# The first norm of a two-layer trunk: row factors before the transposes, gain column behind them

## The chip, the cores and the metric

One NeuronCore of one Trainium2 chip. The metric is device time in microseconds (us) of one execution, median over runs. Engines are named as the profile names them: PE (matmul), PEld (its weight loads), DVE (vector), ACT (scalar), POOL (GpSimd), SP (which issues the DMAs).

## The reference, cut to what matters

```python
def rms_norm(x, gain):
    x32 = x.astype(jnp.float32)
    y = x32 * lax.rsqrt(jnp.mean(x32 * x32, axis=-1, keepdims=True) + RMS_EPS) * gain
    return y.astype(x.dtype)

def swiglu(h, w_gate, w_up, w_down):
    return (jax.nn.silu(h @ w_gate) * (h @ w_up)) @ w_down

h = x                                       # (1, 256, 1024) float32
for layer in range(2):
    g = norm_gain[layer]
    f = swiglu(rms_norm(h, g[0]), w_gate[layer, 0], w_up[layer, 0], w_down[layer, 0])
    h = h + 0.5 * rms_norm(f, g[1])
    ...                                     # a mixer (pooling, or attention), then a second swiglu
```

The width is 1024, the inner width of a swiglu 2816. Only the very first `rms_norm(h, g[0])` and what its output feeds are touched here; four swiglu stages, a pooling mixer, a key/value projection and an attention mixer follow unchanged.

## The kernel before, in words

The 256 tokens are two tiles of 128 rows, `h[0]` and `h[1]`. A float32 product is made of three fast ones: each operand is split into a high part (rounded to the matmul's type) and a low part (the rest), and high·high, high·low and low·high are summed in PSUM. ACT makes the high part, DVE subtracts it to get the low part, both for the weights (`parts` on 1024 columns, lines 99 and 100; `form` on 2048 columns, lines 106 and 107) and for the activations.

A norm is computed with tokens on partitions: ACT squares and sums a row (line 174), DVE adds the two half sums (line 176), POOL raises to the power -1/2 (line 178), DVE multiplies by the gain, which a DMA has spread over all partitions (line 255), and by the row's factor (lines 256 and 260, or ACT on line 258). PE then transposes eight blocks of 128x128 into two PSUM banks of four blocks (`transposed`, line 203); per bank ACT writes the high part (line 205) and DVE the low part (line 206) into `aT`, whose layout is (high or low, block of 128 columns, token).

`Sums` makes four differences of quarters of the transposed activations, split again into parts: the swiglu's products for columns 512 to 2559 use seven half-size products in place of eight, and take these sums as one operand (`st<-hl_hi,S_x`). Before, `add_half` copies three of the four PSUM quarters to SBUF on ACT (line 230), and DVE subtracts (lines 233 to 240); `parts` of that class splits each result (lines 244 and 245).

The first stage of the first swiglu multiplies `aT` by eight weight units (`units`, 1024 columns each, named u0 to u7 below): 96 matmuls into four accumulators `acc_b`, 24 for each token tile and each of gate and up. u0 to u3 are the gate's, u4 to u7 the up's. They come in 1 MB tiles `raw` of two units; three such tiles exist, so the fourth load waits for DVE to have split the first. A unit of index q is multiplied with blocks 2q and 2q+1 of `aT` (modulo four units). Then `pair(1, ...)` begins with the product `g`, from a tile split by `form`.

A scheduler orders most instructions. In the block around the first norm the order of DVE and ACT is that of the code (`manual_schedule`), so an instruction that waits holds up all behind it on its engine. PE's order is the scheduler's. Ahead of all this 64 matmuls on zeros keep PE busy (line 81).

Of the kernel before, what the change touches and what calls it, by code (L numbers as in the profile page):

```python
# [23 lines left out]
NF = FF // P  # L24
KC = D // P
# [5 lines left out]
EPS = 1e-6  # L31
# [13 lines left out]


@with_exitstack
def trunk_kernel(ctx: ExitStack, tc: tile.TileContext, x, pos, gains, pscale, ws, wq, invf, amask, pmat, icnt, out):
# [10 lines left out]
    sc4 = ctx.enter_context(tc.tile_pool(name="sc4", bufs=2))  # L59
    sc2 = ctx.enter_context(tc.tile_pool(name="sc2", bufs=7))  # L60
    sc1 = ctx.enter_context(tc.tile_pool(name="sc1", bufs=1))
    st = ctx.enter_context(tc.tile_pool(name="st", bufs=4))
    accp = ctx.enter_context(tc.tile_pool(name="accp", bufs=4, space=PSUM))
    gup = ctx.enter_context(tc.tile_pool(name="gup", bufs=2, space=PSUM))
    tpp = ctx.enter_context(tc.tile_pool(name="tpp", bufs=2, space=PSUM))

    h = [cp.tile([P, D], F32, name=f"h{i}") for i in range(2)]
    for k in range(2):
        nc.sync.dma_start(h[0][:, k * 512 : (k + 1) * 512], x[0:P, k * 512 : (k + 1) * 512])
    first_units = []  # L70

    ident = cp.tile([P, P], F32, name="ident")
    make_identity(nc, ident)
    nhalf = cp.tile([P, 1], F32, name="nhalf")
# [11 lines left out]
    def load_raw(pool=rawp, tag="raw", raw=None, at=None):  # L86

        b = block_no[0]
        raw = pool.tile([P, 2, 1024], F32, tag=tag, name=f"{tag}{b}") if raw is None else raw
        for k in range(2) if at is None else (at,):  # L90
            last["dma"] = nc.sync.dma_start(raw[:, k], ws[b, :, k * 1024 : (k + 1) * 1024])
        block_no[0] += at != 0
        return raw

    def parts(raw, k, n=1024, xy=False):

        pool, tag = (xyp, "xy") if xy else (hlp, "hl")
        hl = pool.tile([P, 2, 1024], F32R, tag=tag, name="hl")
        nc.scalar.copy(hl[:, 0, :n], raw[:, k, :n])  # L99
        last["dve"] = nc.vector.tensor_sub(hl[:, 1, :n], raw[:, k, :n], hl[:, 0, :n])  # L100
        return hl[:, 0], hl[:, 1]
# [68 lines left out]
    def rstd_of(halves, name):  # L170
        ss = st.tile([P, 2], F32, tag="ss", name=f"ss_{name}")
        for k in range(2):
            jk = sc1.tile([P, 512], BF16, tag="junk", bufs=1, name=f"jk_{name}{k}")
            nc.scalar.activation(jk, halves[k], AF.Square, scale=1.0 / 32.0, accum_out=ss[:, k : k + 1])
        ms = st.tile([P, 1], F32, tag="ms", name=f"ms_{name}")
        nc.vector.scalar_tensor_tensor(ms, ss[:, 0:1], EPS, ss[:, 1:2], op0=ALU.add, op1=ALU.add)
        rs = st.tile([P, 1], F32, tag="rs", name=f"rs_{name}")
        nc.gpsimd.tensor_tensor(rs, ms, nhalf, op=ALU.pow)
        return rs
# [17 lines left out]
    def transposed(i, src, dst, name, sums=None):  # L197

        for b in range(2):
            tp = tpp.tile([P, 4, P], F32, tag="tp", name=f"tp_{name}{i}{b}")  # L200
            for c in range(4):
                k = b * 4 + c
                nc.tensor.transpose(tp[:, c], src[:, k * P : (k + 1) * P], ident)
            d = dst[:, :, b * 4 : b * 4 + 4, i * P : (i + 1) * P]
            nc.scalar.copy(d[:, 0], tp)  # L205
            nc.vector.tensor_sub(d[:, 1], tp, d[:, 0])
            if sums is not None:
                sums.tp[i, b] = tp

    class Sums:  # L210
# [15 lines left out]
        def add_half(self, i, b, tp):  # L226
            a = self.a
            if (i, b) != (1, 1):
                a[i, b] = self.tmp(f"{i}{b}")
                nc.scalar.copy(a[i, b], tp)  # L230
            if (i, b) == (1, 0):
                s3 = self.tmp("s")
                nc.vector.tensor_sub(s3, a[0, 0], tp)
                self.parts(2, s3)
            if (i, b) == (1, 1):
                nc.vector.tensor_sub(a[1, 0], tp, a[1, 0])
                self.parts(0, a[1, 0])
# [3 lines left out]
                self.parts(3, a[0, 1])  # L241

        def parts(self, k, src):
            nc.scalar.copy(self.out[:, k, 0], src)
# [2 lines left out]
    def row_rstd(i, name):  # L247
        return rstd_of([h[i][:, 0:512], h[i][:, 512:1024]], f"q{name}{i}")

    def norm(i, gain, name, rs=None, split=True):  # L250
        rs = row_rstd(i, name) if rs is None else rs
        y = sc4.tile([P, D], F32, tag="y", name=f"n_{name}{i}")
        for k in range(2):
            c = slice(k * 512, (k + 1) * 512)
            nc.vector.tensor_mul(y[:, c], h[i][:, c], gain[:, c])
        nc.vector.tensor_scalar_mul(y[:, 0:512], y[:, 0:512], rs)
        if split:
            nc.scalar.mul(y[:, 512:1024], y[:, 512:1024], rs)
        else:
            nc.vector.tensor_scalar_mul(y[:, 512:1024], y[:, 512:1024], rs)  # L260
        return y
# [4 lines left out]
    def new_aT(name):  # L266
        return atp.tile([P, 2, KC, S], F32R, tag="aT", name=f"aT_{name}")

    def acc_pair(name):
        return [accp.tile([P, 512], F32, tag="acc", name=f"acc_{name}{k}") for k in range(2)]  # L270
# [232 lines left out]
    ivf = cp.tile([P, 32], F32, name="ivf")  # L503
# [33 lines left out]
    aT = go.aT  # L537
# [9 lines left out]
    raw = rawp.tile([P, 2, 1024], F32, tag="raw", name="rawpm")  # L547
# [62 lines left out]
    f = [acc_pair(f"w{i}") for i in range(2)]  # L610
# [38 lines left out]
    aT = go.aT  # L649
# [20 lines left out]
    for g in range(3):  # L670
        units = load_units(4, g % 2 == 0)
        for i in range(2):
# [3 lines left out]
            tp = tpp.tile([P, 4, P], F32, tag="tp", name=f"ktp{g}{i}")  # L676
# [285 lines left out]
```

## Time and profile before

| | us |
|---|---|
| median of three runs | 984.12 (982.98 to 987.3) |
| the profiled execution | 985.76 |
| its span | 984.0 |
| PE busy in the span | 950.4 |
| DVE, ACT, POOL busy in the span | 684.1, 542.9, 62.3 |

The span is from the first to the last instruction on the chip; 1.76 us of the execution lie around it. PE is busy for 97% of the span, so the time that a change at the start can gain or lose is what it does to the moment from which PE runs without a gap, and to later gaps. Busy is not the same as fast: the profile gives for every stretch the clock that PE was granted (PEclk, 1.00 is full speed).

### The profile page before, as it was taken

To read this page: it belongs to the slowest core of one execution; us is meant where nothing else is said; L and a number is where in the kernel's file an instruction comes from. 1 tells how busy PE (TensorE), PEld (TensorE's weight loads), DVE (VectorE), ACT (ScalarE), POOL (GpSimd) and SP (SyncE) were. 2 spreads that over 40 slices of the span, in tenths; PEclk is the share of its full clock that TensorE was granted. 3 is DMA by queue.
4 is the path that set the end of the run, shared out by engine and by line. 5 is a ranking of instruction groups with operands and counts; after the bars stand their busy time and mean duration, and the time that the engine had idled before them with its cause. 6 is when DMAs were issued, how large, how long until landed. Compare 5 with 4: busy or idle time off the path is not lost.

```text
span 984.0 us, 12092 instructions
## 1 busy us (share of the span) xinstructions
PE 950.4 (97%) x4560; PEld 783.7 (80%) x4560; DVE 684.1 (70%) x771; ACT 542.9 (55%) x693; POOL 62.3 (6%) x66
## 2 busy tenths in 40 slices
PE   7999999999999999999999999999987899999997
PEld 6888788878788878877888888788976778887886
DVE  5979874577788886458887964785465587887642
ACT  6665753455657565347656743644345576665531
POOL 0000000000100000000000000100033310000000
PEclk8999999999999999999999999999999799999999
DMA  7886876475468687546687765564324236967721
GB/s 248 286 266 205 259 260 207 173 227 187 164 211 265 181 280 261 179 139 213 153 317 218 268 243 175 177 217 139 127 95 153 86 107 194 330 163 260 247 90 43
DMA packets 55898, 197.16 MB, mean 200 GB/s; under 512 B 7392, under 2 KB 7392, under 8 KB 53792
## 3 DMA queue, kind: packets, MB, share of 16 engines
q1 hardware_dynamic: 53456, 179.35, 52.2%
q0 software_dynamic: 2384, 17.04, 8.9%
q8 instruction: 36, 0.59, 0.2%
q14 instruction: 22, 0.18, 0.0%
HBM read 178.54 MB, written 1.05 MB: 183 GB/s over the span
## 4 chain that ended last, share of the span: by engine, by line
PE 74%; DVE 11%; ACT 5%; DMA 4%; issue 3%; POOL 2%; SPq 0%; POOLq 0%; DVEq 0%; ACTq 0%
PE acc_d L127 22%; PE g L127 12%; PE st L314 12%; PE u L127 7%; PE acc_b L127 6%; PE vp L127 3%; DVE hl L100 3%; PE kp L127 3%; DMA xy<-raw 2%; DVE hl_lo L107 2%; PE htp L295 2%; ACT hl L99 2%; PE qp L127 1%; DVE h L193 1%; PE acc_w L127 1%
## 5 line engine op out<-in xcount | busy, mean ns | idle before, releaser
L100 DVE TENSOR_TENSOR hl<-raw,hl 128x1024 fp32r<-128x1024 f32 x182 | 221.0, 1222 | 111.6 <-ACT hl L99 110.5
L99 ACT CAST hl<-raw 128x1024 fp32r<-128x1024 f32 x182 | 189.7, 1051 | 138.3 <-PE acc_d L127 103.3
L127 PE MATMUL acc_d<-hl,h 128*128 128x512 f32 x1056 | 243.5, 390 | 0.0
L127 PEld LDWEIGHTS acc_d<-hl,h 128*128 128x128 f32 x1056 | 197.3, 188 | 40.4
L107 DVE TENSOR_TENSOR hl_lo<-xy,hl_hi 128x2048 fp32r<-128x2048 f32 x40 | 91.6, 2291 | 48.6 <-ACT hl_hi L106 48.6
L107 DVE TENSOR_TENSOR hl_lo<-raw,hl_hi 128x2048 fp32r<-128x2048 f32 x48 | 109.4, 2285 | 15.6 <-ACT hl_hi L106 15.5
L106 ACT CAST hl_hi<-xy 128x2048 fp32r<-128x2048 f32 x40 | 76.5, 1913 | 64.0 <-DVE xy L333 29.7
L106 ACT CAST hl_hi<-raw 128x2048 fp32r<-128x2048 f32 x48 | 91.9, 1914 | 20.8 <-PE st L314 10.6
L127 PE MATMUL acc_b<-hl,aT_m 128*128 128x512 f32 x192 | 44.8, 392 | 0.3 <-ACT aT_m L205 0.3
L127 PEld LDWEIGHTS acc_b<-hl,aT_m 128*128 128x128 f32 x192 | 35.7, 188 | 8.3 <-ACT aT_m L205 0.8
L127 PE MATMUL g<-hl_hi,aT_m 128*128 128x512 f32 x128 | 41.9, 393 | 0.0
L127 PE MATMUL u<-hl_hi,aT_m 128*128 128x512 f32 x128 | 41.8, 393 | 0.0
L314 PE MATMUL st<-hl_hi,S_m 128*128 128x512 f32 x128 | 41.8, 393 | 0.0
L127 PE MATMUL qp<-hl,aT_f 128*128 128x384 f32 x192 | 38.9, 354 | 0.0
L297 ACT CAST h<-htp 128x512 fp32r<-128x512 f32 (+1 forms) x48 | 26.2, 548 | 20.0 <-PE htp L295 20.0
L127 PEld LDWEIGHTS qp<-hl,aT_f 128*128 128x128 f32 x192 | 34.8, 198 | 1.3 <-issue 0.8
L127 PE MATMUL kp<-hl,aT_hk 128*128 128x512 f32 x144 | 34.6, 394 | 0.0
L331 POOL DMA_DIRECT2D xy<-raw x16 | 14.1, 878 | 305.2 <-DVE xy L333 82.3
L127 PE MATMUL vp<-hl,aT_hk 128*128 128x512 f32 x144 | 33.1, 390 | 0.0
L314 PE MATMUL st<-hl_hi,aT_m 128*128 128x512 f32 x96 | 31.6, 393 | 1.3 <-ACT hl L99 0.9
L721 POOL TENSOR_SCALAR p<-p,rd 128x512 f32<-128x512 f32 x16 | 24.9, 1566 | 121.9 <-DVE rd L720 100.1
L298 DVE TENSOR_TENSOR h<-htp,h 128x512 fp32r<-128x512 f32 (+1 forms) x48 | 30.6, 640 | 1.1 <-ACT h L297 1.0
(246 smaller groups left out, 1596.4 us busy)
## 6 DMA issues: line engine op xcount, KB each, us to landing
raw<-in_ws SPq DMA_DIRECT2D x278, 512.0 KB, 4.8
xy<-in_ws SPq DMA_DIRECT2D x32, 512.0 KB, 6.8
xy<-raw POOLq DMA_DIRECT2D x16, 1024.0 KB, 8.1
rawq<-in_wq SPq DMA_DIRECT2D x8, 768.0 KB, 4.7
gain_post<-in_gains SPq DMA_DIRECT2D x14, 256.0 KB, 5.0
gain_pre<-in_gains SPq DMA_DIRECT2D x12, 256.0 KB, 6.1
rawpm<-in_pmat SPq DMA_DIRECT2D x2, 512.0 KB, 4.1
out_dram<-h SPq DMA_DIRECT2D x4, 256.0 KB, 2.1
```

The lines of the kernel that those rows point to most:

```text
L99: nc.scalar.copy(hl[:, 0, :n], raw[:, k, :n])
L100: last["dve"] = nc.vector.tensor_sub(hl[:, 1, :n], raw[:, k, :n], hl[:, 0, :n])
L106: nc.scalar.copy(hi, raw)
L107: last["dve"] = nc.vector.tensor_sub(lo, raw, hi)
L127: nc.tensor.matmul(o, l, r, start=start, stop=stop)
L193: nc.vector.scalar_tensor_tensor(h[i][:, c], y[:, c], rs, h[i][:, c], op0=ALU.mult, op1=ALU.add)
L295: nc.tensor.transpose(tp[:, k], prod[c, i][:, k * P : (k + 1) * P], ident)
L297: nc.scalar.copy(d[:, 0], tp[:, :nt])
L298: nc.vector.tensor_sub(d[:, 1], tp[:, :nt], d[:, 0])
L314: nc.tensor.matmul(ps, a(z, k), u[v], start=start and k == 0 and n == 0, stop=k == 3 and n == 2, skip_group_check=not start,)
L331: nc.gpsimd.dma_start(dst, src, accum_op=ALU.add)
L721: nc.gpsimd.tensor_scalar_mul(p, p, rd)
```

## The change

The gain of the first norm comes as a column: `gcol` holds 128x8 values, one column for each block, so that it is a factor per partition after the transposes. DVE multiplies `h` by the row factor alone (`first_rows`); `first_transposed` then works block by block: ACT writes the high part of transposed block times gain, DVE the low part with one scalar_tensor_tensor. The squares of a tile are summed half on ACT, half on DVE (`first_rstd`). `add_parts` builds the four quarters for the sums not from PSUM but from the high and low parts in `aT`, with four additions on POOL; the subtractions stay on DVE, and all four now read SBUF. SP's order is written out too.

```diff
+    gcol = cp.tile([P, KC], F32, name="gcol")
+    nc.sync.dma_start(gcol, gain0)          # gains[0].reshape(KC, P).T
...
+        def add_parts(self, aT):
+            a = self.a
+            for i in range(2):
+                for b in range(2):
+                    a[i, b] = self.tmp(f"{i}{b}")
+                    d = aT[:, :, b * 4 : b * 4 + 4, i * P : (i + 1) * P].bitcast(F32)
+                    nc.gpsimd.tensor_add(a[i, b], d[:, 0], d[:, 1])
+            nc.vector.tensor_sub(a[1, 1], a[1, 1], a[1, 0])
+            self.parts(0, a[1, 1])
+            nc.vector.tensor_sub(a[1, 0], a[0, 0], a[1, 0])
+            self.parts(2, a[1, 0])
...
-    gpre = load_gain(0, "pre")
+    def first_rstd(i):
+        ss = st.tile([P, 2], F32, tag="ss", name=f"ss_x{i}")
+        for k in range(2):
...
+            if k == 0:
+                nc.scalar.activation(jk, h[i][:, c], AF.Square, scale=1.0 / 32.0, accum_out=ss[:, 0:1])
+            else:
+                nc.vector.tensor_tensor_reduce(
+                    jk, h[i][:, c], h[i][:, c], 1.0 / 1024.0, 0.0, op0=ALU.mult, op1=ALU.add, accum_out=ss[:, 1:2]
+                )
...
+    def first_rows(i, rs):
+        y = sc4.tile([P, D], F32, tag="y", name=f"n_x{i}")
+        for k in range(2):
+            c = slice(k * 512, (k + 1) * 512)
+            nc.vector.tensor_scalar_mul(y[:, c], h[i][:, c], rs)
+        return y
+
+    def first_transposed(i, y):
+        for b in range(2):
...
+                nc.tensor.transpose(tp[:, c], y[:, k * P : (k + 1) * P], ident)
+            d = aT[:, :, b * 4 : b * 4 + 4, i * P : (i + 1) * P]
+            for c in range(4):
+                g = gcol[:, b * 4 + c : b * 4 + c + 1]
+                nc.scalar.mul(d[:, 0, c], tp[:, c], g)
+                nc.vector.scalar_tensor_tensor(
+                    d[:, 1, c], tp[:, c], g, d[:, 0, c].bitcast(F32), op0=ALU.mult, op1=ALU.subtract
+                )
...
-    with tc.manual_schedule(engines={mybir.EngineType.DVE, mybir.EngineType.Activation}):
-        y = norm(0, gpre, "x")
+    with tc.manual_schedule(engines={mybir.EngineType.DVE, mybir.EngineType.Activation, mybir.EngineType.SP}):
         raws = [load_raw(at=0)]
-        first_units += [parts(raws[0], 0, xy=True)]
+        load_raw(at=1, raw=raws[0])
         nc.sync.dma_start(h[1], x[P:, :])
-        transposed(0, y, aT, "x", sums)
-        rs = row_rstd(1, "x")
-        load_raw(at=1, raw=raws[0])
-        first_units += [parts(raws[0], 1, xy=True)]
-        y = norm(1, gpre, "x", rs, False)
         raws.append(load_raw())
-        first_units += [parts(raws[1], 0)]
-        transposed(1, y, aT, "x", sums)
-        first_units += [parts(raws[1], 1)]
-    for i in range(2):
-        sums.add(i)
+        rs = first_rstd(0)
+        u0 = xyp.tile([P, 2, 1024], F32R, tag="xy", name="hl")
+        nc.scalar.copy(u0[:, 0], raws[0][:, 0])
+        y = first_rows(0, rs)
+        nc.vector.tensor_sub(u0[:, 1], raws[0][:, 0], u0[:, 0])
+        first_transposed(0, y)
+        u1 = parts(raws[0], 1, xy=True)
+        rs = first_rstd(1)
+        u2 = parts(raws[1], 0)
+        y = first_rows(1, rs)
+        first_transposed(1, y)
+        first_units += [(u0[:, 0], u0[:, 1]), u1, u2, parts(raws[1], 1)]
+    sums.add_parts(aT)
```

How the change moves the queues is seen in the programs' orders, engine by engine. First DVE, from the low part of u1 to that of u3, before (`raw_199` holds u0 and u1, `raw_237` u2 and u3; names after "waits" are the engines or DMA semaphores that must have counted up):

```order
L100 TENSOR_TENSOR hl<-raw_199,hl 128x1024 [waits DMAHW6_49,Activation_49]
L255 TENSOR_TENSOR n_x_232<-h_101,gain_pre_178 128x512 [waits DMAHW5_49]
L255 TENSOR_TENSOR n_x_232<-h_101,gain_pre_178 128x512
L256 TENSOR_SCALAR n_x_232<-n_x_232,rs_qx_226 128x512 [waits DVE_49,Pool_49]
L260 TENSOR_SCALAR n_x_232<-n_x_232,rs_qx_226 128x512 [waits DVE_49]
L100 TENSOR_TENSOR hl<-raw_237,hl 128x1024 [waits DMAHW7_49,Activation_49]
L206 TENSOR_TENSOR aT_x<-tp_x_243,aT_x 128x4x128 [waits Activation_49]
L206 TENSOR_TENSOR aT_x<-tp_x_250,aT_x 128x4x128 [waits Activation_49]
L100 TENSOR_TENSOR hl<-raw_237,hl 128x1024 [waits DMAHW0_49,Activation_49]
L233 TENSOR_TENSOR sum_xs<-sum_x_261,tp_x_243 128x512 [waits Activation_49]
```

And now (`raw_184` holds u0 and u1, `raw_188` u2 and u3; ISA is the squaring with its sum):

```order
L102 TENSOR_TENSOR hl<-raw_184,hl 128x1024 [waits DMAHW4_49,Activation_49]
L509 ISA jk_x_238,ss_x_235<-h_101 128x512 [waits DMAHW5_49]
L509 ISA ss_x_235 128x1
L513 SCALAR_TENSOR_TENSOR ms_x_240<-ss_x_235 128x1 [waits DVE_49,Activation_49]
L102 TENSOR_TENSOR hl<-raw_188,hl 128x1024 [waits DMAHW6_49,Activation_49]
L522 TENSOR_SCALAR n_x_247<-h_101,rs_x_242 128x512 [waits Pool_49]
L522 TENSOR_SCALAR n_x_247<-h_101,rs_x_242 128x512
L536 SCALAR_TENSOR_TENSOR aT_x<-tp_x_250,gcol,aT_x 128x128 [waits Activation_49] x4
L536 SCALAR_TENSOR_TENSOR aT_x<-tp_x_263,gcol,aT_x 128x128 [waits Activation_49] x4
L253 TENSOR_TENSOR sum_x_286<-sum_x_286,sum_x_284 128x512 [waits Pool_49]
L102 TENSOR_TENSOR hl<-raw_188,hl 128x1024 [waits DMAHW7_49,Activation_49]
```

The sum of squares of tile 1 (row `ms`) now stands behind the low part of u1 and a squaring of DVE's own; eight small instructions stand where two large ones stood; and the first subtraction for the sums, which waits for POOL, has come ahead of the low part of u3.

ACT, from the first high part of a unit, before (the square of tile 1 is `jk_qx`):

```order
L99 CAST hl<-raw_199 128x1024 [waits DMAHW4_49]
L205 CAST aT_x<-tp_x_205 128x4x128 [waits PE_49]
L205 CAST aT_x<-tp_x_212 128x4x128 [waits PE_49]
L174 ACTIVATE jk_qx_220,ss_qx_219<-h_101 128x512 [waits DMAHW5_49,Activation_49]
L174 ACTIVATE jk_qx_222,ss_qx_219<-h_101 128x512 [waits Activation_49]
L99 CAST hl<-raw_199 128x1024 [waits DMAHW6_49]
L99 CAST hl<-raw_237 128x1024 [waits DMAHW7_49]
```

And now:

```order
L549 CAST hl<-raw_184 128x1024 [waits DMAHW3_49]
L535 ACTIVATE aT_x<-tp_x_206,gcol 128x128 [waits DMAHW2_49,PE_49]
L535 ACTIVATE aT_x<-tp_x_206,gcol 128x128 [waits DVE_49] x3
L535 ACTIVATE aT_x<-tp_x_219,gcol 128x128 [waits PE_49]
L535 ACTIVATE aT_x<-tp_x_219,gcol 128x128 [waits DVE_49] x3
L101 CAST hl<-raw_184 128x1024 [waits DMAHW4_49]
L507 ACTIVATE jk_x_236,ss_x_235<-h_101 128x512 [waits DMAHW5_49,Activation_49]
L101 CAST hl<-raw_188 128x1024 [waits DMAHW6_49]
```

Each block's high part, but for the first of a bank, waits for DVE (it has read the same bank for the block before); the high part of u1 and the square of tile 1 stand behind all eight, where the square stood behind two instructions that waited for PE alone.

On POOL the program before has two small instructions here, the powers for the row factors of tile 0 and tile 1. Now it has six: power, two additions for tile 0, power for tile 1, two additions for tile 1. Beyond the first 60 us the orders of all engines are the same.

More of the change, by code (lines that the diff above doesn't have):

```diff
@@ L47, in trunk_kernel @@
 @with_exitstack
-def trunk_kernel(ctx: ExitStack, tc: tile.TileContext, x, pos, gains, pscale, ws, wq, invf, amask, pmat, icnt, out):
+def trunk_kernel(ctx: ExitStack, tc: tile.TileContext, x, pos, gains, gain0, pscale, ws, wq, invf, amask, pmat, icnt, out):
     nc = tc.nc
@@ L241, in add_half @@
                 self.parts(3, a[0, 1])
+        def add_parts(self, aT):
[9 more added lines that the diff above has]
+            self.parts(2, a[1, 0])
+            nc.vector.scalar_tensor_tensor(a[0, 0], a[0, 0], -1.0, a[1, 1], op0=ALU.mult, op1=ALU.subtract)
+            self.parts(1, a[0, 0])
+            nc.vector.scalar_tensor_tensor(a[0, 1], a[0, 1], -1.0, a[0, 0], op0=ALU.mult, op1=ALU.subtract)
+            self.parts(3, a[0, 1])
         def parts(self, k, src):
@@ L480, in __call__ @@
             self.third(i)
-    gpre = load_gain(0, "pre")
+    def first_rstd(i):
+        ss = st.tile([P, 2], F32, tag="ss", name=f"ss_x{i}")
+        for k in range(2):
+            c = slice(k * 512, (k + 1) * 512)
+            jk = sc1.tile([P, 512], BF16, tag=f"junk{k}" if k else "junk", bufs=1, name=f"jk_x{i}{k}")
+            if k == 0:
[4 more added lines that the diff above has]
+                )
+        ms = st.tile([P, 1], F32, tag="ms", name=f"ms_x{i}")
+        nc.vector.scalar_tensor_tensor(ms, ss[:, 0:1], EPS, ss[:, 1:2], op0=ALU.add, op1=ALU.add)
+        rs = st.tile([P, 1], F32, tag="rs", name=f"rs_x{i}")
+        nc.gpsimd.tensor_tensor(rs, ms, nhalf, op=ALU.pow)
+        return rs
@@ new lines, in first_rows @@
+    def first_rows(i, rs):
+        y = sc4.tile([P, D], F32, tag="y", name=f"n_x{i}")
+        for k in range(2):
+            c = slice(k * 512, (k + 1) * 512)
+            nc.vector.tensor_scalar_mul(y[:, c], h[i][:, c], rs)
+        return y
+    def first_transposed(i, y):
+        for b in range(2):
+            tp = tpp.tile([P, 4, P], F32, tag="tp", name=f"tp_x{i}{b}")
+            for c in range(4):
+                k = b * 4 + c
+                nc.tensor.transpose(tp[:, c], y[:, k * P : (k + 1) * P], ident)
+            d = aT[:, :, b * 4 : b * 4 + 4, i * P : (i + 1) * P]
+            for c in range(4):
+                g = gcol[:, b * 4 + c : b * 4 + c + 1]
[3 more added lines that the diff above has]
+                )
@@ L939 @@
         "gains": gains,
+        "gain0": gains[0].reshape(KC, P).T,
         "pscale": i["pool_scale"][0],
```

## The prediction

> **What bounds the kernel now.** I read the page's busy line first, then the chain of waits of the first 60 us, then the clock there, then the timeline of the start. The page says that PE is nearly always busy, so a change at the start is worth what it does to the moment from which PE runs without a gap.
>
> ```profile
> PE 950.4 (97%) x4560; PEld 783.7 (80%) x4560; DVE 684.1 (70%) x771; ACT 542.9 (55%) x693; POOL 62.3 (6%) x66
> ```
>
> The chain of waits (start, length, what) shows which work set that moment:
>
> ```profile
> 2.11 6.92 DMA gain_pre<-in_gains
> ...
> 14.88 1.23 DVE hl L100
> ...
> 16.16 2.61 PE acc_b L127 x6
> ...
> 19.24 0.59 ACT aT_x L205
> ...
> 19.88 19.11 PE acc_b L127 x83
> 38.99 2.72 PE g L127 x12
> ```
>
> The spread gain lands at 9.03 us (2.11 + 6.92) and holds up the norm of tile 0; from 16.16 on the chain is PE. After tile 1's transposes PE runs 83 matmuls in a row, 0.230 us each, and is done with the first stage at 38.99. I call that moment E: everything behind it is the same program, so its shift is the forecast. The six matmuls from 16.16 took 0.43 us each, which the stretches of 1 us explain (busy PE, PEld, DVE, ACT, POOL; then the granted clock, the DMA share and GB/s):
>
> ```profile
> 11.00:12.00 1.00, 0.37 (x4) 0.13 (x2) 0.40 (x1) 1.00 (x3) 0.00 (x0) 0.71 1.01 414
> 14.00:15.00 1.00, 1.00 (x4) 0.72 (x3) 0.22 (x3) 1.00 (x2) 0.56 (x1) 0.50 1.02 414
> 18.00:19.00 1.00, 1.00 (x7) 0.84 (x6) 1.00 (x2) 0.00 (x0) 0.00 (x0) 0.87 0.79 221
> ```
>
> The clock is halved from about 11.5 to 18.3. The timeline gives the rest of the start:
>
> ```profile
> 0.98 5.46 PE L81 MATMUL warm<-zeros 128*128 128x128 bf16 x64 [0.98 <-DVE zeros L78]
> 4.34 0.63 ACT L174 ACTIVATE jk_qx<-h 128x512 bf16<-128x512 f32 x1
> 5.09 0.16 DVE L176 SCALAR_TENSOR_TENSOR ms_qx<-ss_qx 128x1 f32<-128x1 f32 x1 [4.17 <-ACT jk_qx L174]
> 5.41 0.55 POOL L178 TENSOR_TENSOR rs_qx<-ms_qx,nhalf 128x1 f32<-128x1 f32 x1 [4.11 <-DVE ms_qx L176]
> 10.27 1.10 PE L203 MATMUL tp_x<-ident,n_x 128*128 128x128 f32 x8 [3.83 <-DVE n_x L256]
> 14.19 0.56 POOL L178 TENSOR_TENSOR rs_qx<-ms_qx,nhalf 128x1 f32<-128x1 f32 x1 [8.23 <-DVE ms_qx L176]
> 17.23 0.48 DVE L256 TENSOR_SCALAR n_x<-n_x,rs_qx 128x512 f32<-128x512 f32 x1
> 17.62 0.48 DVE L260 TENSOR_SCALAR n_x<-n_x,rs_qx 128x512 f32<-128x512 f32 x1
> 18.61 1.04 PE L203 MATMUL tp_x<-ident,n_x 128*128 128x128 f32 x8
> 19.86 1.29 DVE L206 TENSOR_TENSOR aT_x<-tp_x,aT_x 128x512 fp32r<-128x512 f32 x2 [0.62 <-ACT aT_x L205]
> 21.30 1.23 DVE L100 TENSOR_TENSOR hl<-raw,hl 128x1024 fp32r<-128x1024 f32 x1
> 29.03 0.69 DVE L245 TENSOR_TENSOR S_x<-sum_x,S_x 128x512 fp32r<-128x512 f32 x1 [1.23 <-ACT S_x L244]
> 30.24 2.35 DVE L100 TENSOR_TENSOR hl<-raw,hl 128x1024 fp32r<-128x1024 f32 x2
> ```
>
> The last row is the low parts of u6 and u7, done at 32.59. PE needs u7's for the last twelve matmuls, at 38.99 - 2.72 = 36.27. So DVE is 3.7 us ahead of PE: a delay of DVE up to that costs nothing, the rest costs in full. That slack is what the change plays with.
>
> **The prices.** From the groups (count, busy and mean ns) and one stretch of alternating ACT and DVE:
>
> ```profile
> L593 DVE SCALAR_TENSOR_TENSOR yT<-yp,psc,yT 128x256 fp32r<-128x256 f32 x8 | 3.8, 480 | 1.4 <-ACT yT L592 1.4
> L592 ACT ACTIVATE yT<-yp,psc 128x256 fp32r<-128x256 f32 x8 | 3.7, 474 | 3.5 <-PE yp L127 2.0 <-DVE yT L593 1.4
> L749 DVE TENSOR_TENSOR oT<-ob,oT 128x128 fp32r<-128x128 f32 x8 | 2.3, 290 | 10.2 <-ACT oT L748 10.2
> L748 ACT CAST oT<-ob 128x128 fp32r<-128x128 f32 x8 | 2.1, 260 | 3.8 <-PE ob L127 3.8
> L710 DVE CUSTOM_DVE_ANT_0 p<-sc,qT 128x512 f32<-128x512 f32 x16 | 10.9, 685 | 5.6 <-PE sc L127 5.3 <-issue 0.3
> L721 POOL TENSOR_SCALAR p<-p,rd 128x512 f32<-128x512 f32 x16 | 24.9, 1566 | 121.9 <-DVE rd L720 100.1 <-ACT qT L737 15.0 <-PE qtp L770 6.9
> 237.48 0.48 ACT L592 ACTIVATE yT<-yp,psc 128x256 fp32r<-128x256 f32 x1 [0.55 <-DVE yT L593]
> 237.99 0.48 DVE L593 SCALAR_TENSOR_TENSOR yT<-yp,psc,yT 128x256 fp32r<-128x256 f32 x1 [0.54 <-ACT yT L592]
> ```
>
> Lines 592 and 593 are the new pair of instructions on blocks twice as wide, and they alternate strictly, 0.03 us between them. No row has the pair on 128x128. Bounds for one step (ACT, DVE, two hops): 0.61 from the plain pair L748 and L749, 1.02 from L592 and L593 as they are. I take 0.78: the wide pair less 128 elements at about 1 ns each, which leaves 0.36 and 0.35. A tile takes 8 steps, less the 0.38 that the bank change overlaps: 5.9 us, against 1.9 before (two casts and two subtractions from 19.24 to 21.15). An addition on POOL has no row either: 0.55 (a one-column operation) below, 3.1 (twice the one-input row) above; I take 1.57, that row.
>
> POOL and DVE disturb each other:
>
> ```profile
> 195.44 1.22 DVE L100 TENSOR_TENSOR hl<-raw,hl 128x1024 fp32r<-128x1024 f32 x1
> 195.60 1.47 POOL L178 TENSOR_TENSOR rs_qf<-ms_qf,nhalf 128x1 f32<-128x1 f32 x1 [3.94 <-DVE ms_qf L176]
> 712.96 3.12 POOL L721 TENSOR_SCALAR p<-p,rd 128x512 f32<-128x512 f32 x2 [75.93 <-DVE rd L720]
> 714.62 1.40 DVE L100 TENSOR_TENSOR hl<-rawq,hl 128x768 fp32r<-128x768 f32 x1 [1.05 <-ACT hl L99]
> L100 DVE TENSOR_TENSOR hl<-rawq,hl x16: 943/958/1396, 685.5 to 743.6; 128x768 fp32r<-128x768 f32 x16
> ```
>
> A power of 0.55 us takes 1.47 behind a low part on DVE; a low part of 0.95 us takes 1.40 beside a POOL operation. So I charge +0.9 and +0.45 where they meet. The Trainium skill, SBUF — State Buffer, "Who interferes with whom", says that a DVE instruction with two SBUF inputs and a GpSimd one that reads SBUF exclude each other, the second blocking fully; the power agrees, the 768-column low part shows half of it. By that rule the sum below would be about 0.6 us longer.
>
> **The change, step by step** (times in us of the span).
>
> 1. *Tile 0's norm.* The halves of `h[0]` are there by 4.1 or so (the second square starts at 4.34 without a wait). DVE's square takes 0.685 and some 0.08 to read out; the row factor is ready at 5.7 in place of 5.96. No gain is waited for: the two scalings end at 6.2 and 6.6, and the transposes follow the warm-up's end at 6.5, in place of 10.27: 3.8 us of lead. The column `gcol` is a small transfer ahead of the weights; I cost it at nothing, since the first weights are needed only behind the norm.
> 2. *Weights.* Half a megabyte fewer goes ahead of them. At the 414 GB/s of the rows above 512 KB take 1.27 us, so from 4.1 on the halves land at about 5.4 (u0), 6.7 (u1), 7.9 (`h[1]`), 9.2 and 10.4. None is waited for. Removed with it: two gain multiplications per tile.
> 3. *Tile 0's turn.* u0's low part stands ahead on DVE (6.5 to 7.8). The alternation then runs from 7.7 to 13.0. PE does six matmuls and is idle from about 9.5.
> 4. *The hold-up of tile 1.* u1's high part, landed at 6.7, stands behind ACT's eight blocks: 12.6 to 13.6. Its low part follows; POOL's second addition runs then: 13.6 to 15.2. Behind it on DVE the square of tile 1 (to 15.9), the sum (16.1), then u2's low part at once, so that the power takes the long form: 16.2 to 17.8, in place of 14.19 to 14.75. Scalings to 18.7 (before 18.1), transposes at 18.3 (before 18.61). The lead of 3.8 is spent.
> 5. *Tile 1's turn.* First block 19.4 (PE is slow, see 7), last low part 25.1; before, 21.15.
> 6. *The sums.* POOL's last addition runs from 25.2 to 26.8. The first subtraction waits for it at the head of DVE's queue, with u3's low part behind it. From there to u7's low part the set of twelve instructions is the same as before (five low parts, four differences, three split-offs). Before it took from 21.30 to 32.59, 1.2 of it waiting for ACT (row 29.03); I allow 0.6 of waiting: 10.7, so u7 is done at 37.5, 4.9 later than before.
> 7. *PE.* u7 alone would put E at 37.5 + 2.7 = 40.2. Stricter is u3's low part, at 28.6: of the 83 matmuls 27 can run before it (tile 1 and the rest of tile 0 with u0 to u2, and four that need only high parts), 56 cannot: 28.6 + 56 × 0.228 = 41.4. The clock adds little: PE rests 4 us from 9.5, longer than the 3.83 after which it fell before, and I let it come back after as long as before (12.1 to 18.3), at 25; then 11 of the 27 matmuls take 0.43, the others run until 28.7, and E is 41.5.
>
> Sum: 41.5 - 38.99 = +2.5. The three copies that ACT no longer makes buy nothing: ACT's turn in this stretch is set by DVE, with which it alternates, and by the weights. Behind E DVE is late by 4 while PE is late by 2.5; I find the later low parts just in time, and charge nothing for them (0 to 0.5). Only from a page: the Trainium skill, GPSIMD Engine Reference, has 4497 ns for an addition of 2048 columns; a quarter, 1.12 us as an estimate, would make the sum +1.8.
>
> The profiled execution took 985.76, its span 984.0; the median of the runs is 984.12. The shift applied to the median gives 986.6.
>
> **The rivals.**
>
> - *Faster: the early start holds.* If a step of the alternation costs the lower 0.61, both tiles' turns are 1.35 shorter; if POOL's addition is below 1 us, DVE's wait in step 6 shrinks by a further 1. Then u3's low part is ready by 24.5, nothing waits for DVE, and PE goes through tile 1 from about 17.5: 17.5 + 1 + 83 × 0.23 = 37.6, 1.4 faster: 982.7. For it: the 13 early matmuls at half clock cost 2.6 more than at full clock, and the gain is no longer waited for. Against it: the strict alternation, and the row factor of tile 1 behind u1 and u2. To gain 4.9 u7 must be split by 31.4, so twelve instructions earlier (20.7) tile 1 must be through; its row factor would have to come before 14, which step 4 excludes unless ACT is through tile 0 by 10.
> - *Slower: POOL.* Additions of 3.1 and full exclusion: u1's low part waits until 16.2 (+2.2), the last addition ends 1.9 later, E = 45.6: +6.6, 990.7. It decides from an addition of about 2.5 us on.
> - *No change: the slack takes it.* DVE's lateness stays under 3.7 (step 0.68, addition 1.2): E within 1 us of 38.99, 984.1.
>
> **How the numbers follow.** A difference under 0.5% (4.9 us) is about what a measurement of this kernel can't tell from none. The forecast, a loss of 1 to 4.5, gets 0.45 and has 985 to 988.7 as its own range; no change 0.17; faster 0.18, of which 0.06 pass 4.9; slower through POOL, or through late low parts behind E, 0.2, of which nearly all pass it. The range for eight in ten goes from 981.3 (twice the gain of the early start) to 990.8 (the POOL case). Faster 0.06, same 0.74, slower 0.20.
>
> **What would show it.** In the profile after: tile 0's transposes near 6.5; ACT and DVE in turns of 0.78 us; u1's high part after tile 0's last block, near 12.6; tile 1's power near 16 and longer than 1 us; its transposes near 18; an addition on POOL of about 1.6 us and a DVE wait for it of 1 to 2 us near 25; u7's low part near 37.5; the first `g` matmul at 41.5. I am wrong if the alternation is quicker, if tile 1's power comes before 15, or if DVE does not wait for POOL.

## The result and the profile after

The changed kernel takes 990.04 us (median of seventeen runs) against 984.12 for the kernel before. One of the seventeen was disturbed; the other sixteen lie between 986.84 and 992.92 us, and by them the kernel takes 1.0056 times as long, 95% interval 1.0045 to 1.0068. It is slower by about 5.5 us; the bound of 0.5% from the prediction lies inside the interval. The forecast was 986.6.

The profiled execution, 986.84 us with a span of 985.1, is the fastest of the sixteen, which matters below. The page's busy line hardly moves:

```profile
PE 949.8 (96%) x4560; PEld 781.0 (79%) x4560; DVE 686.6 (70%) x784; ACT 542.3 (55%) x697; POOL 67.9 (7%) x70
```

The chain of waits does (start, length, what), up to the place where PE takes it over:

```profile
2.11 4.70 DMA raw<-in_ws
6.84 1.06 ACT hl L549
...
13.89 1.04 ACT hl L101
14.96 1.85 DVE hl L102
16.81 0.60 DVE jk_x L509
17.77 1.51 POOL rs_x L515
19.30 0.50 DVE n_x L522
19.84 1.13 PE tp_x L531 x4
...
26.79 1.31 POOL sum_x L252
28.12 0.70 DVE sum_x L253
...
36.58 1.96 DVE hl L102 x2
...
39.45 3.90 DVE hl_lo L109 x2
...
60.91 1.19 PE st L333 x4
```

Before, the chain began with the spread gain (landed at 9.03) and was PE's from 16.16 on. Now it begins with the first half of the first weight tile (u0), goes through the two turns, waits for POOL twice (the power of tile 1, the last addition), and stays with DVE and ACT until 60.91.

The timeline (start, length, engine, line, operation; in brackets the idle time ahead and what ended it):

```profile
5.20 0.55 POOL L515 TENSOR_TENSOR rs_x<-ms_x,nhalf 128x1 f32<-128x1 f32 x1 [3.90 <-DVE ms_x L513]
6.84 1.05 ACT L549 CAST hl<-raw 128x1024 fp32r<-128x1024 f32 x1 [2.65 <-DMA raw<-in_ws]
9.84 0.35 DVE L536 SCALAR_TENSOR_TENSOR aT_x<-tp_x,gcol,aT_x 128x128 fp32r<-128x128 f32 x1 [0.43 <-ACT aT_x L535]
10.23 0.37 ACT L535 ACTIVATE aT_x<-tp_x,gcol 128x128 fp32r<-128x128 f32 x1 [0.42 <-DVE aT_x L536]
14.46 1.27 POOL L252 TENSOR_TENSOR sum_x<-aT_x 128x512 f32<-128x512 f32 x1 [1.35 <-DVE aT_x L536]
14.96 1.85 DVE L102 TENSOR_TENSOR hl<-raw,hl 128x1024 fp32r<-128x1024 f32 x1 [0.58 <-ACT hl L101]
28.12 0.69 DVE L253 TENSOR_TENSOR sum_x<-sum_x,sum_x 128x512 f32<-128x512 f32 x1 [1.41 <-POOL sum_x L252]
28.73 1.22 DVE L102 TENSOR_TENSOR hl<-raw,hl 128x1024 fp32r<-128x1024 f32 x1
30.00 13.28 PE L129 MATMUL acc_b<-hl,aT_x 128*128 128x512 f32 x56 [1.00 <-DVE hl L102]
43.12 0.39 PE L129 MATMUL g<-hl_hi,aT_x 128*128 128x512 f32 x1
```

ACT has nothing to do for 2.65 us until u0 lands. Then ACT and DVE alternate, 0.79 us a block. PE waits 1.00 us for u3's low part, does the last 56 matmuls of the first stage from 30.00 on and reaches `g` at 43.12. Before, the same row stood 4.3 us earlier:

```profile
38.83 0.39 PE L127 MATMUL g<-hl_hi,aT_x 128*128 128x512 f32 x1
```

The first power of the next norm, 150 us on, shows what is left of it; before, then after:

```profile
191.10 0.56 POOL L178 TENSOR_TENSOR rs_pf<-ms_pf,nhalf 128x1 f32<-128x1 f32 x1 [89.74 <-DVE ms_pf L176]
```

```profile
195.83 0.56 POOL L180 TENSOR_TENSOR rs_pf<-ms_pf,nhalf 128x1 f32<-128x1 f32 x1 [89.77 <-DVE ms_pf L178]
```

4.73 us, and the code from there on is the same. Yet the spans differ by 1.1 only. In the second swiglu the shift falls from 4.7 to 3.4 us: the profile before has 1.3 us more of PE standing still there. That differs from execution to execution: a run below that starts the same (x6_gcol_behind) keeps 4.6. In the attention stage (640 to 785 us) it falls by another 2.5, with a granted clock of 0.94 before and 0.98 after; one stretch of 20 us of it, before and after (the column ahead of the DMA share is the granted clock):

```profile
760.00:780.00 20.00, 16.54 (x91) 13.28 (x93) 9.91 (x26) 9.27 (x20) 6.21 (x4) 0.76 0.39 135
```

```profile
760.00:780.00 20.00, 13.66 (x78) 10.32 (x80) 10.84 (x28) 10.43 (x24) 6.20 (x4) 0.91 0.56 200
```

So two spans are a poor measure of a change at the start; below I use the moment of the first `g` row and the row of `rs_pf`.

### The profile page after: what moved, and what is told of

The parts are those of the page before. It is cut to its first block, busy times and chain, and to the rows that moved or that the text cites. A ratio compares the mean times of both kernels' runs of the same rounds, so it can differ in the third digit from the quotient of the medians.

```text
span 985.1 us, 12102 instructions
## 1 busy us (share of the span) xinstructions
PE 949.8 (96%) x4560; PEld 781.0 (79%) x4560; DVE 686.6 (70%) x784; ACT 542.3 (55%) x697; POOL 67.9 (7%) x70
## 4 chain that ended last, share of the span: by engine, by line
PE 71%; DVE 13%; ACT 6%; issue 4%; POOL 2%; DMA 2%; SPq 0%; DVEq 0%; POOLq 0%; ACTq 0%
PE acc_d L129 22%; PE st L333 12%; PE g L129 10%; PE u L129 7%; PE acc_b L129 4%; PE vp L129 3%; DVE hl L102 3%; PE kp L129 3%; DVE hl_lo L109 2%; PE qp L129 2%; ACT hl L101 2%; PE htp L314 1%; PE acc_w L129 1%; PE acc_u L129 1%; DVE h L195 1%
## 5 line engine op out<-in xcount | busy, mean ns | idle before, releaser
L129 PEld LDWEIGHTS acc_d<-hl,h 128*128 128x128 f32 x1056 | 197.2, 188 | 40.5
L129 PE MATMUL acc_b<-hl,aT_x 128*128 128x512 f32 x96 | 26.6, 429 | 7.1 <-ACT hl L101 4.2
L333 PE MATMUL st<-hl_hi,aT_m 128*128 128x512 f32 x96 | 31.3, 392 | 0.3 <-DVE c L390 0.3
```

The source lines that it names most:

```text
L129: nc.tensor.matmul(o, l, r, start=start, stop=stop)
L333: nc.tensor.matmul(ps, a(z, k), u[v], start=start and k == 0 and n == 0, stop=k == 3 and n == 2, skip_group_check=not start,)
```

## The experiments

Theories for the loss beyond the forecast, with the letters of the expectations. A: the queues of the two turns and what they hold up. B: POOL's additions for the sums. C: the half clock, which PE falls into because it now rests early. D: the landing of u0, which before was hidden behind the gain and is now first in the chain.

The results in one table. "u0" is the start of ACT's first high part, which in every kernel but the first waits only for the landing; "g" the first `g` row; "g - u0" what lies between; `rs_pf` the row above. All times in us; a ratio is against the kernel before on the same chip, with its 95% interval. The runs went to several chips, so compare them by the ratios and not by the medians. The code cuts below are shortened.

| run | u0 | g | g - u0 | rs_pf | median, runs | ratio |
|---|---|---|---|---|---|---|
| before | (10.54) | 38.83 | | 191.10 | 984.12 | |
| after | 6.84 | 43.12 | 36.28 | 195.83 | 990.04, 17 | 1.0056 (1.0045 to 1.0068) |
| x1_banks | 9.38 | 42.34 | 32.96 | 195.03 | 988.39, 10 | 1.0028 (1.0013 to 1.0043) |
| x2_u3first | 9.46 | 44.83 | 35.37 | 197.34 | 990.69, 4 | 1.0054 (1.0033 to 1.0075) |
| x3_noadd | 6.36 | 41.52 | 35.16 | 194.57 | 989.31, 5 | 1.0050 (1.0034 to 1.0066) |
| x7_filler | 7.94 | 44.93 | 36.99 | 197.29 | 990.74, 4 | 1.0055 (1.0037 to 1.0074) |
| x4_norm1_early | 9.73 | 44.73 | 35.00 | 197.76 | 990.10, 4 | 1.0063 (1.0041 to 1.0085) |
| x6_gcol_behind | 6.82 | 43.10 | 36.28 | 195.80 | 989.03, 5 | 1.0058 (1.0038 to 1.0078) |
| x8_hold | 8.17 | 45.31 | 37.14 | 197.65 | 990.06, 4 | 1.0062 (1.0040 to 1.0084) |
| x9_all | 7.43 | 38.75 | 31.32 | 191.27 | 986.44, 12 | 1.0017 (1.0002 to 1.0032) |
| x11_hold2 | 6.98 | 43.27 | 36.29 | 196.05 | 988.54, 8 | 1.0036 (1.0023 to 1.0050) |
| x12_best | 6.65 | 38.54 | 31.89 | 191.94 | 986.86, 12 | 1.0017 (1.0008 to 1.0026) |
| x13_nohold | 8.50 | 39.31 | 30.81 | 192.71 | 987.48, 12 | 1.0020 (1.0006 to 1.0034) |
| x14_order | 6.42 | 39.03 | 32.61 | 191.62 | 985.72, 12 | 1.0010 (0.9999 to 1.0022) |

**The turn through two banks (x1_banks).** Both banks are transposed first; then block c of one, block c of the other.

```diff
-        for b in range(2):
-            tp = ...; (four transposes); d = ...
-            for c in range(4):
+        (tps, ds of both banks)
+        for c in range(4):
+            for b in range(2):
                 nc.scalar.mul(...); nc.vector.scalar_tensor_tensor(...)
```

> The blocks are taken in turn from the two PSUM banks, so that ACT can write a block of one bank while DVE reads the other. Theory A (the turns: ACT and DVE alternate on one bank, 0.79 us a block, and tile 1's turn ends late): a turn falls from 6.6 us to 8 x 0.39 + 0.4 = 3.5, twice on the path, so u3's low part is ready some 5 us sooner (about 25 in place of 29.95), and E, the first g matmul, comes at 39.5 to 40.5 in place of 43.1, then bound by PE, whose clock is halved when tile 1 starts; time 986 to 987. Theory B (POOL's additions at the head of DVE's queue set E): the wait for them stays, E falls by less than 1.5. Theory C (the halved clock sets E): E falls by less than 1.

Tile 1's turn in the timeline, and the square of tile 1 ahead of it:

```profile
21.57 3.16 ACT L539 ACTIVATE aT_x<-tp_x,gcol 128x128 fp32r<-128x128 f32 x8 [4.91 <-PE tp_x L532]
16.65 1.76 DVE L509 CUSTOM_DVE_ANT_0 jk_x<-h 128x512 bf16<-128x512 f32 x1
```

Eight blocks run without a gap, 3.16 us; the wait for the neighbour (0.42 us a block) is gone, so it came from the shared bank, not from the data. Counted from the landing `g` comes 3.3 us sooner, as A said (about 3); the moment itself, 42.34, missed A's 39.5 to 40.5, since u0 landed 2.5 us later in this profile. The time falls all the same. Part of what the turns gave was lost again: the two additions of a tile now come together and meet the square, 1.76 us where it takes 0.69 alone. On the shared bank the Trainium skill, PSUM — Partial Sum Buffer, "PSUM bank collisions raise a hardware error", says that two engines may not touch one bank in the same partitions at once and that software puts a dependency between them; the trace agrees, 0.79 us a block against 0.40.

**u3's low part ahead of the subtraction that waits for POOL (x2_u3first).**

```diff
-    sums.add_parts(aT)
+    with in_turn("dve"):
+        sums.add_parts(aT)
```

> The subtractions for the sums are queued on DVE behind u3's low part, not ahead of it. Theory A with step 6 of the prediction (u3's low part waits behind POOL's last addition): u3's low part starts at 27.3 in place of 28.73, E falls by 0.8 to 1.4 to about 42. Theory C: E unchanged at 43.1.

```profile
29.69 1.86 DVE L102 TENSOR_TENSOR hl<-raw,hl 128x1024 fp32r<-128x1024 f32 x1 [0.58 <-ACT hl L101]
```

The wait for POOL is off u3's path, but the low part now runs beside the addition, 1.86 us for 1.22. Of 1.41 us of waiting 0.9 remain as gain at `g`; the time did not fall.

**No additions at all (x3_noadd).** The sums are made from the high parts alone, so POOL adds nothing.

```diff
-                    nc.gpsimd.tensor_add(a[i, b], d[:, 0], d[:, 1])
+                    (d[i, b] = the high part itself, as operand of the subtractions)
```

> Leaves out the four additions on POOL: the sums are made from the high parts alone (low parts of the quarters left out). Theory A: u1's low part no longer meets POOL (1.85 to 1.22 us), and the first subtraction no longer waits (1.4 us): E falls by 2.0 to about 41.1, time by 2. Theory B: all of the 4.3 goes, E at 39 or below. Theory C: E unchanged or down by less than 0.5.

```profile
30.96 10.72 PE L129 MATMUL acc_b<-hl,aT_x 128*128 128x512 f32 x46 [0.35 <-DVE hl L102]
```

`g - u0` falls by 1.1 us, where A said 2.0 and B 4.3. PE no longer stops for u3 but a little for u4's low part, which is why it is no more. B is worth 1.1 us and can't be the main cause.

**A clock that doesn't fall (x7_filler).** Fourteen matmuls that nobody reads, behind tile 0's fourth block.

```diff
+        for _ in range(14):
+            nc.tensor.matmul(warm, aT[:, 0, 3, 0:P], u0[:, 0, 0:512], start=True, stop=True)
         u1 = parts(raws[0], 1, xy=True)
```

> Adds 14 matmuls of 512 columns on data that is there (their result is not used) behind tile 0's first six, in the stretch where PE rested, so that the clock does not fall. Theory A: the clock stays up to tile 1's turn or falls later, but u3's low part stays at 28.7 to 30, so E moves by less than 0.4. Theory C: the matmuls before u3 are quicker and E falls by 1.5 to 2.5.

Stretches of 1 us, after and in this run (granted clock third from the end):

```profile
16.00:17.00 1.00, 0.14 (x1) 0.14 (x1) 1.00 (x2) 0.48 (x1) 0.00 (x0) 0.50 0.00 0
```

```profile
16.00:17.00 1.00, 0.49 (x1) 0.19 (x1) 0.94 (x1) 1.00 (x4) 0.83 (x1) 1.00 0.00 0
```

The clock is full there. Counted from u0, u3's low part was done 0.5 us sooner (22.65 us against 23.11), and PE still stood 0.99 us for it: up to there a full clock is worth 0.5 us and not the 1.5 to 2.5 of C. Yet `g` came 0.7 us later, for now the clock fell behind that wait: 0.72, 0.50, 0.50 and 0.58 in the four stretches of 1 us from 30 on, and the last 56 matmuls took 14.46 us in place of 13.28. C is not the main cause in the kernel as changed, but the clock is not free either.

**Tile 1's norm in the middle of tile 0's turn (x4_norm1_early).**

```diff
-        first_transposed(0, y)
+        first_transposed(0, y, lambda: rs1.append(first_rstd(1)))   # between the banks
+        y = first_rows(1, rs1[0])
         u1 = parts(raws[0], 1, xy=True)
-        rs = first_rstd(1)
         u2 = parts(raws[1], 0)
-        y = first_rows(1, rs)
```

> Tile 1's squares, its sum and its power stand between the two banks of tile 0's turn, and tile 1's two row products right behind that turn, ahead of the second and third weight parts. Theory A (the queues of the two turns and what is held up between them make the loss): the wait for the power (0.45 us, behind 0.8 us of squares and sum and 1.2 us of a low part) goes, but the two low parts, 1.2 us each, now stand between the rows and DVE's half of tile 1's turn; g starts 1.5 to 2 us sooner counted from the landing of the first weight half than in the changed kernel (there 36.28 us), that is 34.3 to 34.8, and the time is about 988.3 where the landing is like the others'. Theory D (it is the landing of the first weight half alone that makes the loss): g stands as far behind the landing as before, 36.3, time unchanged at 990.

1.3 us counted from u0, just short of A's 1.5 to 2. Tile 1's rows meet an addition:

```profile
18.92 1.89 DVE L522 TENSOR_SCALAR n_x<-h,rs_x 128x512 f32<-128x512 f32 x2
```

The landing was the latest of all, at 9.7, and the time did not fall.

**The small transfer of the gain behind u0 (x6_gcol_behind).**

```diff
-    nc.sync.dma_start(gcol, gain0)
...
         raws = [load_raw(at=0)]
+        nc.sync.dma_start(gcol, gain0)
```

> The 4 KB of gain, which go as 1024 small pieces of 4 bytes, are asked for behind the first weight half and no longer ahead of it. If those small pieces hold up the first weight half (one form of theory D), it lands 4 us or less after its issue, at 5.5 to 6.2 us, and the time falls by 1.5 to 2.5 us to about 988. If they don't, it lands 4.2 to 7.3 us after its issue as in the five profiles so far, and the time stays within 1 us of 990; the gain must then land before the first turn, at 7 to 9.5 us, or it holds up the turn itself.

u0 at 6.82 and `g` at 43.10, the same as after to 0.02 us. It was asked for 0.45 us sooner and landed 5.1 us after its issue, within the spread of the others; the time did not move measurably. The small transfer is not the cause.

**Holding the loads behind u0 (x8_hold, x11_hold2).** First with tile 1's rows of x still travelling beside it, then with nothing behind it.

```diff
-        load_raw(at=1, raw=raws[0])
         nc.sync.dma_start(h[1], x[P:, :])
-        raws.append(load_raw())
         rs = first_rstd(0)
+        nc.gpsimd.tensor_copy(raws[0][:, 1, 0:1], raws[0][:, 0, 0:1])
+        load_raw(at=1, raw=raws[0])
+        raws.append(load_raw())
```

> GpSimd copies one column from the first weight half to the place of the second, ahead of the second half's load, so that this load and all behind it are asked for only when the first half has landed; tile 1's rows of x are asked for ahead of it. Theory D (the first half lands late, and now late and now early, since what was asked for behind it shares the engines): it lands 3.5 to 4.5 us after its issue, at 5.5 to 6.5 us; the second half lands about 5 us later, at 11 to 12, still ahead of the 13.9 at which ScalarE takes it; g comes at 42 to 42.7 us and the time falls by 2 to 3 us to about 987.5, with a smaller spread. If the sharing is not the cause, the landing stays between 4.2 and 7.3 us after its issue and the time at 990 or above it, for the loads behind come later.

```diff
         rs = first_rstd(0)
+        nc.gpsimd.tensor_copy(h[1][:, 0:1], raws[0][:, 0, 0:1])
         nc.sync.dma_start(h[1], x[P:, :])
         load_raw(at=1, raw=raws[0])
```

> The changed kernel with tile 1's rows of x and every weight load but the first half held until that half has landed (GpSimd writes one column into the place of tile 1's rows, from the landed half). In the run with the first hold the 512 KB of tile 1's rows still travelled beside the half, and it took 6.0 us. Theory D (transfers asked for behind the half share the rate of 250 to 350 GB/s with it): with nothing behind it, it lands 3 to 4 us after its issue, at 5 to 6 us, in every run; g, 36.3 us later, at 41.5 to 42.5, and the time falls by 2 to 3 us to 987 to 988, unless the loads that now come 3 us later bring a wait of the matmuls (0.9 us in the run with the first hold). If sharing is not the cause the landing stays at 6 to 9.5 us and the time at 990 or above.

The DMA view of the first 2.3 us: u0's load, count, size and us from issue to landing. First of after, then of x2_u3first, x8_hold and x11_hold2:

```profile
raw<-in_ws SPq DMA_DIRECT2D x1, 512.0 KB, 4.7
```

```profile
raw<-in_ws SPq DMA_DIRECT2D x1, 512.0 KB, 7.3
```

```profile
raw<-in_ws SPq DMA_DIRECT2D x1, 512.0 KB, 6.0
```

```profile
raw<-in_ws SPq DMA_DIRECT2D x1, 512.0 KB, 4.8
```

Without a hold the nine profiles have 4.7, 7.2, 7.3, 4.2, 5.8, 7.6, 5.1, 5.3 and 6.4; with nothing behind the load the three (x11, x12, x14) have 4.8, 4.5 and 4.3. The first hold did not do it (6.0). `g` came late there for another reason: the clock was halved from 31.3 to 34.7, and the 56 matmuls took 14.59 us. (The wait of 0.9 us that the second expectation ascribes to later loads is PE's wait for u3's low part, 0.99 there and 1.00 in after.) With the second hold the spread of the landing is gone in three profiles, though 4.3 to 4.8 us is still more than the 3 to 4 expected. The time fell by some 2.0 us by the ratios ((1.0056 - 1.0036) × 984). Their intervals just overlap (1.0045 to 1.0050), so the gain is likely and not certain. D is borne out for the spread of the landing; its mean price rests on this run and on the sum below.

**Together (x9_all, x12_best, x13_nohold, x14_order).** Banks in turn, tile 1's norm in the middle of tile 0's turn, u3's low part first:

> Three changes together: the turns go through the two banks alternately, tile 1's squares, sum and power stand in the middle of tile 0's turn and its rows right behind it, and the fourth weight low part stands ahead of the first subtraction of the sums. Theory A: from the landing of the first half tile 0's turn ends after 7.2 us, the rows after 8.8, two low parts after 11.3, tile 1's turn after 14.8, the fourth low part after 16, and g starts 29 to 31 us behind the landing, for the last low part then bounds it (36.28 in the changed kernel). With a landing at 7 to 9 us g comes at 36.5 to 39.5, against 38.8 in the kernel before, and the time is 982.5 to 985. Theory D alone: about 988 to 990.

```profile
16.84 22.07 PE L129 MATMUL acc_b<-hl,aT_x 128*128 128x512 f32 x90
13.14 2.87 DVE L522 TENSOR_SCALAR n_x<-h,rs_x 128x512 f32<-128x512 f32 x2
```

Counted from u0 `g` comes 5.0 us sooner, at 31.3, just outside A's 29 to 31. 90 matmuls run without a stop (at half clock until 19.8), `g` is at 38.75 as in the kernel before, and `rs_pf` 0.2 behind it. So what the turns and the hold-ups between them had cost is given back; D alone would have left `g` 36.3 behind u0. The time stays 0.17% above before's, where A said 982.5 to 985.

Then, on top of it, eleven filler matmuls and tile 1's additions ahead of tile 0's (`for i in (1, 0)`), with the second hold and without:

> The three changes together of the run before, with the hold of the run beside this, with eleven 512-wide matmuls whose result nobody reads behind tile 0's first products (they keep TensorE busy in the 3.2 us before tile 1's transposes), and with tile 1's two additions for the sums ahead of tile 0's, so that none runs beside tile 1's rows. In the run of the three together g came 31.3 us behind the landing, 90 matmuls took 22.07 us where 0.227 each make 20.4, and tile 1's two rows took 2.87 us beside an addition, 1.76 without. Theory A and D: the clock gives 1.6, the rows 1.1, so g comes 28.6 us behind a landing at 5 to 6 us, at 34 to 35, 4 us sooner than in the kernel before: 979 to 981. Theory C refuted for good (the clock is never worth anything): g 30.2 behind the landing, 981 to 983. D wrong: the landing at 7 to 9.5, 982 to 984.

> The same as the run beside it without the hold. g 28.6 us behind the landing, which wanders between 6.3 and 9.7 as in the nine profiles so far: g at 35 to 38.3, time 981 to 984 with a wider spread than with the hold. If the hold costs more by later loads than it gives, this one is the faster of the two.

Both missed the 28.6: `g` came 31.89 and 30.81 us behind u0, at 38.54 and 39.31. Two of the four additions now ran beside the first subtraction and the low part behind it:

```profile
22.97 1.77 DVE L253 TENSOR_TENSOR sum_x<-sum_x,sum_x 128x512 f32<-128x512 f32 x1 [1.20 <-POOL sum_x L252]
24.66 2.31 DVE L102 TENSOR_TENSOR hl<-raw,hl 128x1024 fp32r<-128x1024 f32 x1
```

0.69 and 1.22 alone: what tile 1's rows no longer lost, these did. And behind `g` it is DVE that sets the pace: in x12 it reached the first gate's product at 41.5 (40.1 before), so `rs_pf` is 0.8 behind before though `g` came 0.3 sooner; in x13 `rs_pf` is 1.6 behind. The two show no gain in time from the hold: u0 landed 1.85 us sooner with it, `g` came only 0.77 sooner, since DVE and ACT now waited 0.2 to 0.9 us for tile 1's rows and for u2, and the ratios, 1.0017 and 1.0020, can't be told apart. So the old order of additions once more, with fillers and hold:

> The run of everything with the hold, but with the additions for the sums in the order of the changed kernel, tile 0's first. There the first subtraction stood beside an addition (1.77 us, 0.69 alone), the low part behind it too (2.31, 1.22 alone), DVE reached the gate's product of the first block at 41.5 (40.1 in the kernel before), and behind the first g the matmuls waited for it, so the time was 986.9 though g came no later than before. Theory A: with tile 0's additions beside tile 1's rows again (1.1 us more there) but none beside the subtraction, g 30 us behind a landing at 5.5 to 6.7, at 36 to 37, the gate's product at 37.5 to 39, time 982.5 to 984 against 985 for the kernel before. If the order is worth nothing, 986 to 987 as there.

985.72 against 984.39 beside it, 1.0010 (0.9999 to 1.0022): the same as before, which neither reading expected (`g` at 39.03 and not 36 to 37, DVE's product at 41.3 and not 37.5 to 39). The eleven fillers ran at half clock:

```profile
12.09 5.06 PE L562 MATMUL warm<-hl,aT_x 128*128 128x512 f32 x11 [1.67 <-ACT aT_x L541]
```

and so ended 2.2 us later than at full clock (5.06 - 2.82, their time in x12). Tile 1's transposes stood behind them on PE and began at 16.95, though the rows were ready at 15.50. No version here beats the kernel before; these four come within 0.2% of it.

## Why the prediction was right or wrong

The sign was right and the time within the wide range; the likeliest value was 3.4 us too low, mostly by one term, and the time lies above the forecast's own 985 to 988.7. That the wide range held it is in part luck: its upper end, 990.8, stood for long additions on POOL, which did not come. The forecast's shift was +2.5; the profile shows +4.3 at `g` and the medians +5.9.

1. *Tile 0's norm*: right. Power at 5.20, transposes at 6.92 (6.5 forecast).
2. *Weights*: this step failed. "None is waited for", with u0 landing at 5.4, 3.3 us after its issue: from 4.1 on, alone, at 414 GB/s. ACT waited for it until 6.84. The stretch from 5 to 6 us, after and in x14, where nothing else is under way (the last number is GB/s):

```profile
5.00:6.00 1.00, 1.00 (x13) 1.00 (x11) 0.26 (x2) 0.00 (x0) 0.55 (x1) 1.00 0.75 287
5.00:6.00 1.00, 1.00 (x21) 1.00 (x19) 0.20 (x3) 0.00 (x0) 0.53 (x1) 1.00 0.52 209
```

Even alone the load got about half of the 414, a rate read from a stretch with several loads under way, and landed 4.3 to 4.8 us after its issue in the three runs with the hold. In the profile after it was 4.7, so there the missing 1.4 us are the rate and not the loads behind; those come on top in other profiles, up to 7.6. Everything after is late by about that amount: the end of tile 0's turn 14.4 for 13.0, the transposes 19.84 for 18.3, u3's low part done at 29.95 for 28.6, `g` 43.12 for 41.5.
3. *Tile 0's turn*: right, 0.79 a step for 0.78.
4. *The hold-up of tile 1*: right in order and size. u1's low part took 1.85 beside the addition (1.6 charged), tile 1's power 1.50 as charged, at 17.77.
5. *Tile 1's turn*: right, 21.00 to 26.71, 5.7 us for 5.7.
6. *Sums*: POOL's additions took 1.26 to 1.30 for 1.57. The estimate of 1.12 by the Trainium skill, GPSIMD Engine Reference, "Elementwise — side-by-side cycle accounting", was nearer, 0.14 to 0.18 too low. The wait of the first subtraction came as told, 1.41.
7. *PE*: right to the count, 56 matmuls behind u3's low part, 0.234 each for 0.228. The clock was halved from 12.8 to 23.0 and cost 0.5 us at tile 1's transposes, as x7 shows; step 5 had allowed for that.
8. *Behind E*: from 4.3 at `g` to 4.73 at `rs_pf`, 0.4 within the 0 to 0.5 allowed; charging nothing was the wrong end.

The sum with the measured terms: 2.5 + 1.4 by u0 + 0.4 of small terms (among them 0.16, because the forecast counted from the chain's 38.99 and the row stands at 38.83, and 0.3 by the 56 matmuls) = 4.3 at `g`; + 0.4 behind it = 4.7. For the usual run: the nine profiles without a hold have u0 at 8.05 on the mean, 1.2 later than the profile after: 4.7 + 1.2 = 5.9, against 5.9 between the medians and 5.5 by the ratio. That the runs without a profile land like the nine profiles is an inference; their traces don't exist.

Of the rivals "slower: POOL" came closest in time (990.7), for a wrong reason: additions of 3.1 us did not exist. "The early start holds" needed steps of 0.61; x1 reached 0.40 by using two banks, and with the norm of tile 1 moved up (x9) the early start just made good what it had cost. The exclusion between DVE and POOL was charged with 0.9 us for a power and only 0.45 for a low part. The experiments show more: a square 0.69 to 1.76, a power 0.55 to 1.50, and in x12 a low part 1.22 to 2.31, which agrees with the Trainium skill, SBUF — State Buffer, "Who interferes with whom"; in the changed kernel itself it cost 0.6 on u1's low part and 0.95 on the power.

## What to carry to other kernels

Taking away the first wait of a chain puts the next one in its place: ask when the second thing lands, from rows where it is not hidden, and don't compute the landing of a single load from the rate that many loads reach together. ACT and DVE in turns on one PSUM bank ran one after the other (0.79 us a block); on two banks they overlapped (0.40). Additions moved to the idle POOL were paid for on DVE, so count what runs beside each addition.

## What was not expected of the hardware

- A 512 KB load issued at 2.11 us (1.65 in x6) landed 4.2 to 7.6 us later when other loads were issued behind it, and 4.3 to 4.8 when none was. Alone it moved at 209 GB/s (x14, 5 to 6 us), where several loads together moved at 414.
- The mean granted clock of an execution goes with almost as much time as this change cost: of the kernel before, seven runs with a mean granted clock of 0.985 average 986.97 us, eighteen at 0.992 average 983.04.
- The same short rest can halve the clock or not. In x12 and x14 PE rested 1.76 and 1.67 us at the same place, behind the same work; the stretch from 12 to 13 us reads, x12 first:

```profile
12.00:13.00 1.00, 0.61 (x3) 0.52 (x4) 0.82 (x4) 1.00 (x3) 0.12 (x1) 1.00 0.84 225
```

```profile
12.00:13.00 1.00, 0.91 (x2) 0.81 (x3) 0.93 (x3) 1.00 (x3) 0.50 (x1) 0.50 0.90 279
```

The Trainium skill, TensorE: Matmul & The Clock Gate, "What's actually happening", says that the window in which activity is judged, some 3.4 us long, runs free of the kernel's start. The granted clocks by the microsecond agree with such a window: every stretch at half clock in the first 60 us lasts a multiple of 3.4 us (3.4 in x7 and in the second stretch of x8; 6.8 in before, x3, x6, x9, x11 and x14; 10.2 in after, x1, x2 and the first of x8; 13.6 in x4). PE need not rest for all of it: in the 3.4 us ahead of the fall it was busy for 1.9 us in x14 and 1.6 in x7. Why x12 kept its clock would follow if its windows lay elsewhere; no row shows where they lie while the clock stays full.
